# From the cross attention on: scheduler's order of the compute engines replaced by program order, with one list of weight splits

## The chip, the core and the metric

The kernel runs on one core of a Trainium2 chip. TensorE (PE) does the matmuls, VectorE (DVE), ScalarE (ACT) and GpSimd (POOL) the rest, and SyncE (SP) issues the loads. The metric is the device time of one execution in microseconds; the kernel before takes 1673.18 us (median of three runs, 1670.4 to 1673.23).

## What is computed

One layer of a first model and two layers of a second, on 256 tokens of width 1024, all in float32:

```python
# first block
y = concat(conformer_conv(p), rwkv7_mix(p)) @ w_out;          x = x + rms_norm(y, g1)
y = memory_cross_attention(rms_norm(x, g2), mem_n, wq, wkv, wo);  x = x + rms_norm(y, g3)
y = swiglu(rms_norm(x, g4), w_gu, w_down);                    x = x + rms_norm(y, g5)
# second block, layer 0 (mixer: moba attention) and layer 1 (mixer: mamba2)
x = x + 0.5 * swiglu(rms_norm(x, f1), gate, up, down)
x = x + mixer(rms_norm(x, mx))
x = x + 0.5 * swiglu(rms_norm(x, f2), gate, up, down)
```

So behind the first mixing come, in this order: cross attention, FFN (2816 wide), FFN, moba attention, FFN, FFN, mamba2, FFN. The mamba2 mixer projects to z and x (2048 each), B and C (1024 each) and 32 steps, runs a causal convolution of four taps and silu over x, B and C, a chunked scan of 32 heads in 8 groups, gates with silu(z), norms each group, and projects back.

## The kernel before, in words

**Matmuls and splits.** Each float32 product is made of three fp32r matmuls: high part by high part, high by low, low by high. So every weight unit (128x2048 float32, 1 MB) is loaded by SP into one of three raw buffers (pools `praw` and `pr8`) and split in two halves of 1024 columns: a cast on ACT into `wh` (L205, or L198 for units made `ahead`) and a subtraction on DVE into `wl` (L207, L199); some units of the mamba2 part subtract on POOL. The pool `pw` holds four halves; an `ahead` unit goes into two buffers of the pool of seven big tiles instead. Activations are split in the same way (`split`, L314 and L316).

**Order.** From the first weave on, PE's instructions are in program order (`manual_schedule` with PE alone). ACT, DVE, POOL and SP are ordered by the compiler's scheduler, which may put a later instruction first; `high_priority` marks those that it is to prefer.

**FFN.** `ffn` runs eleven chunks of 256 columns: eight steps of gate and up (`wide_step`, six 512-column matmuls, three for each half of the tokens), silu and product (`evict`, L1104 and L1105), four PE transposes of the chunk before (`turned`), and the down projection of the chunk before (`down_steps`). In chunks 0 and 10 the two halves of the tokens come one after the other.

**The boundary between two parts.** `down_two` does the last two down units, first for token half 0, then for half 1. `Fin.done(th, o)` adds the result to x: one DVE addition (L432) where there is no gain (`post` is None), or squares on ACT, a root on POOL and two products and two additions on DVE (L439 to L450) where there is one. `PreT.turn(th, q)` makes the next part's input: four PE transposes into one PSUM bank (L391), then for each of the four blocks a product on ACT (`xh`, L397) and a subtraction on DVE (`xl`, L398), then a square on ACT (L383). Half 0 is turned inside `down_two`; the two turns of half 1 (`late`) come in the next part, after its steps 1 and 3 (no gain) or 5 and 7 (gain), and at the very start of the mamba2 part.

**Weave.** `weave(fill, chains)` lays out attention and mixer: each step takes the next piece of the projections (`fill`), then one step of every chain that is due; a chain's `yield n` says after how many steps it goes on. In the mamba2 part a step of fill is twelve matmuls of 256 columns, and a group g starts eight steps after the group before it.

**A mamba2 group** (`group`): `conv_unit` (a product L1429 on DVE, two ACT products L1432, six DVE taps, L131), tanh (L1453) and a product (L1454), eight ACT relus and two exps (L1467, L1468) from PE's broadcasts, the masked B-C product (L1475 to L1479), the gate (L1484, L1485), PE transposes of x and the scaled copies (L1496 to L1499), PE's products with the masks (`by`) and the carried state (`bo`), sums (L1517 to L1520), squares (L1523), a root on POOL (L1524 to L1527), the norm on ACT (L1529), PE transposes of y (L1534), and the split of the result (L1540, L1541).

Of the kernel before, what the change touches and what calls it, by code (L numbers as in the profile page):

```python
# [97 lines left out]
def _build(ctx, nc, tc, a):  # L98
# [112 lines left out]

    def lin_step(bk, u, xh, xl, k, m, last=7):
        h, l = u
# [6 lines left out]
    def lin_pair(bks, us, xh, xl, k, last=7):  # L220

        for lo_ in (False, True):
# [17 lines left out]
    def linT_step(bk, u, xh, xl, k):  # L240
        h, l = u[0][k // 4], u[1][k // 4]
# [13 lines left out]
    def wide_step(bks, us, xh, xl, k, halves=(0, 1)):  # L255

        h, l = us[k // 4]
# [9 lines left out]
    def down_part(acc, u, hh, hl, th, o, k, first, last):  # L267
        t, c = slice(th * 128, th * 128 + 128), slice(o * 512, o * 512 + 512)
        h, l = u[0][k][:, c], u[1][k][:, c]
# [5 lines left out]
    def down_two(acc, u, yu, v, yv, fin):  # L275


        for th in range(2):
            hh, hl = yu(th)
            for o in range(2):  # L280
                for k in range(2):
                    down_part(acc, u, hh, hl, th, o, k, False, False)
            yield
            if th and fin.post is None:
                fin.turn(0, 0)
                fin.turn(0, 1)
            hh, hl = yv(th)
            for o in range(2):
# [3 lines left out]
                if th and fin.post is not None:  # L292
                    fin.turn(0, o)
                yield
# [179 lines left out]
    def weave(fill, chains):  # L474
# [4 lines left out]
        while due or fill:  # L479
            if fill and next(fill[0], "end") == "end":  # L480
                fill.pop(0)
                if fill:
                    continue
            left = []
# [8 lines left out]
            n += 1  # L493

# [453 lines left out]
    order.__enter__()  # L948
    yc = split(y_c[1])
# [3 lines left out]
    uq = unit(a["wq"][0]), unit(a["wq"][1])  # L953
# [5 lines left out]
    psa = mkpool("psa", 4, space=PSUM)  # L959

    def outs_of(n, l, get, nfs, nx, fins, nxt, post, acc):

        acc.extend(new_acc())
        for g in range(l - 2):
            yield from down_steps(acc, unit(a[n][g], True), lambda: get[g], g == 0)
        u, v = unit(a[n][l - 2], True), unit(a[n][l - 1], True)
        nfs.extend(two(*nx)())
        fins.append(Fin(xt, acc, nxt, post))
        yield from down_two(acc, u, lambda th: get[l - 2], v, lambda th: get[l - 1], fins[0])

    def two(n, l):
        return lambda: (unit(a[n][l * 22], True, ahead=True), unit(a[n][l * 22 + 1]))


    def softmax_T(bk, scale_ap):
# [18 lines left out]
    def first_heads():  # L994
        qb[0].append(bank())
        qb[1].append(bank())
        for k in range(8):
            lin_pair((qb[0][0], qb[1][0]), uq, xh, xl, k)
# [4 lines left out]
    def mem_head(h):  # L1003
# [7 lines left out]
        Pn = softmax_T(bk, r16)  # L1011
        yield 2
# [14 lines left out]
    acc, nf = [], []  # L1027
# [5 lines left out]
    def rope_tables():  # L1033
# [27 lines left out]

        ang = reduce_angle(ang, 2 * math.pi * 4096.0)
        ang = reduce_angle(ang, 2 * math.pi)
        rr = s1()[:, 0:128]
# [7 lines left out]
        S.activation(sn[:, 128:256], ab2, AF.Sin)  # L1072
        for n in ("qn", "kn"):
            cg = s1("v").rearrange("p (h t) -> p h t", h=2)
# [9 lines left out]
    for h in (2, 3):  # L1084
        fill.append(pieces(lambda h=h: unit(a["wq"][h], True), qb[h]))
    fill.append(outs_of("wo", 4, oh, nf, ("wgu", 0), fins, nxt2, "g3r", acc))
# [3 lines left out]
    def ffn(wgu, wd, l, pre, nf, before, nxt, post=None, ahead=None):  # L1090

# [6 lines left out]
        pend = None  # L1098
# [15 lines left out]
        last = []  # L1114

        def turned_last(th):
# [5 lines left out]
            with tc.high_priority():  # L1122
                split(bk[:, :, 0:128], "f", last[0][:, :, t], last[1][:, :, t])

        def gate_up(c):
            return unit(a[wgu][l * 22 + 2 * c], True, ahead=True), unit(a[wgu][l * 22 + 2 * c + 1], True)

        us10 = None
        for c in range(11):
            us = nf if c == 0 else us10 or gate_up(c)  # L1130
            b = bank(), bank()
            if c in (0, 10):
                for th in range(2):
                    for k in range(8):
                        wide_step(b, us, xh, xl, k, (th,))
# [6 lines left out]
                    if c == 0 and th == 0:  # L1142
                        r = pre.r()
                        ru = r
                        if post is None:
                            ru = small(2)
                            V.tensor_scalar(ru, r, 0.5, None, MUL)
                    evict(c, b[th], th)
            else:
                for k in range(8):  # L1150
                    wide_step(b, us, xh, xl, k)
# [4 lines left out]
            if c == 9:  # L1156
                us10 = gate_up(10)
            d = unit(a[wd][l * 11 + c], True)
            if 0 < c < 10:
                run(down_steps(acc, pend, lambda: hl, c == 1))  # L1160
            if c < 10:
                pend = d
        nf = ahead() if ahead else None
        fin = Fin(xt, acc, nxt, post)

        def last_but_one(th):
            if th:
# [3 lines left out]
        run(down_two(acc, pend, last_but_one, d, lambda th: last, fin))  # L1171
        return nf, fin
# [3 lines left out]
    nf, fin = ffn("wgu", "wdn", 0, pre, nf, fin, nx, "g5r", two("f1gu", 0))  # L1176
    pre, nx = nx, PreT("mx", 0)
    nf, fin = ffn("f1gu", "f1d", 0, pre, nf, fin, nx, None,
                   lambda: (unit(a["wqk"][0], True, ahead=True), unit(a["wqk"][1])))
# [64 lines left out]
    def pair(j):  # L1244
# [11 lines left out]
        for e in range(2):  # L1256
# [11 lines left out]
            S.activation(sm[:, 128:384], sm[:, 128:384], AF.Exp, bias=mx[:, 1:2], scale=SC, accum_out=su[:, 1:2])  # L1268
            V.reciprocal(su, su)
# [3 lines left out]
            yield E2 if e else 1  # L1273
# [25 lines left out]
    nf2, acc, fins = [], [], []  # L1299
    nx2 = PreT("f2", 0)  # L1300

    fill = [wide(lambda: nf, qk[0], late_, True)]
# [349 lines left out]
```

## Time and profile before

| | |
|---|---|
| median of three runs | 1673.18 us (1670.4 to 1673.23) |
| the profiled execution's own time | 1672.08 us |
| its span, first to last instruction | 1670.2 us |
| PE busy | 1605.0 us (96%) |
| DVE busy | 1062.8 us (64%) |
| ACT busy | 864.9 us (52%) |
| POOL busy | 148.5 us (9%) |
| mean granted PE clock | 0.988 |

Busy time is the union of an engine's instructions. A PE that is busy can run at the full clock of 2.4 GHz (1.00) or at half of it (0.50); the stretches at half clock are in the column PEclk of the windows. Parts, by the loads and lines of the trace: cross attention about 268 to 332 us, FFN to 527, FFN to 721, moba to 837, FFN to 1027, FFN to 1219, mamba2 to 1477, FFN to the end.

### The profile page before, as it was taken

To read this page: it belongs to the slowest core of one execution; us is meant where nothing else is said; L and a number is where in the kernel's file an instruction comes from. 1 tells how busy PE (TensorE), PEld (TensorE's weight loads), DVE (VectorE), ACT (ScalarE), POOL (GpSimd) and SP (SyncE) were. 2 spreads that over 40 slices of the span, in tenths; PEclk is the share of its full clock that TensorE was granted. 3 is DMA by queue.
4 is the path that set the end of the run, shared out by engine and by line. 5 is a ranking of instruction groups with operands and counts; after the bars stand their busy time and mean duration, and the time that the engine had idled before them with its cause. 6 is when DMAs were issued, how large, how long until landed. Compare 5 with 4: busy or idle time off the path is not lost.

```text
span 1670.2 us, 21978 instructions
## 1 busy us (share of the span) xinstructions
PE 1605.0 (96%) x8702; PEld 1374.4 (82%) x8702; DVE 1062.8 (64%) x1649; ACT 864.9 (52%) x1437; POOL 148.5 (9%) x162
## 2 busy tenths in 40 slices
PE   7999999999999999999999999999999888999999
PEld 7898988878887888877878887888898887778887
DVE  7888856655456555477565555555569888765454
ACT  6734446654345444466654445444466665554442
POOL 2322200000000000001000000000022433000000
PEclk9999999999999999999999999999999999999999
DMA  8321234354544445442454544545434322455442
GB/s 284 127 77 51 102 119 170 132 211 153 222 154 177 182 171 204 174 167 99 163 181 174 201 175 177 182 173 203 174 104 165 136 101 102 151 202 193 185 177 76
DMA packets 39846, 265.98 MB, mean 159 GB/s; under 512 B 4672, under 2 KB 5440, under 8 KB 8384
## 3 DMA queue, kind: packets, MB, share of 16 engines
q1 hardware_dynamic: 39456, 263.41, 43.4%
q8 instruction: 68, 1.11, 0.3%
q10 hardware_dynamic: 288, 1.18, 0.2%
q14 instruction: 34, 0.28, 0.1%
HBM read 263.52 MB, written 1.05 MB: 158 GB/s over the span
## 4 chain that ended last, share of the span: by engine, by line
PE 74%; DVE 14%; ACT 6%; issue 3%; POOL 1%; DMA 0%; SPq 0%; POOLq 0%; DVEq 0%; ACTq 0%
PE bk L181 71%; DVE wl L207 3%; DVE s2w L131 2%; ACT wh L205 2%; PE bk L1111 1%; DVE cv L131 1%; ACT s2w L1467 1%; DVE s2f L1519 1%; DVE s2f L1520 1%; ACT s L397 1%; PE bk L751 1%; PE bk L391 1%; DVE s2n L1429 1%; ACT s2w L1432 0%; DVE s L398 0%
## 5 line engine op out<-in xcount | busy, mean ns | idle before, releaser
L181 PE MATMUL bk<-wh,s 128*128 128x512 f32 (+1 forms) x2400 | 745.0, 384 | 14.7 <-ACT s L397 6.1
L207 DVE TENSOR_TENSOR wl<-raw,wh 128x1024 fp32r<-128x1024 f32 x344 | 422.7, 1234 | 265.7 <-ACT wh L205 264.9
L181 PEld LDWEIGHTS bk<-wh,s 128*128 128x128 f32 x2400 | 443.6, 191 | 108.3 <-DVE s L398 16.0
L205 ACT CAST wh<-raw 128x1024 fp32r<-128x1024 f32 x366 | 381.8, 1051 | 286.9 <-PE bk L181 266.4
L181 PE MATMUL bk<-wl,s 128*128 128x512 f32 (+1 forms) x1200 | 450.9, 376 | 1.3 <-POOL wl L207 1.3
L181 PE MATMUL bk<-wh,s2f 128*128 128x512 f32 x1072 | 345.6, 392 | 0.0
L181 PEld LDWEIGHTS bk<-wl,s 128*128 128x128 f32 x1200 | 229.2, 191 | 38.6 <-POOL wl L207 1.5
L181 PEld LDWEIGHTS bk<-wh,s2f 128*128 128x128 f32 x1072 | 201.2, 188 | 41.7 <-DVE s2f L316 0.2
L181 PE MATMUL bk<-s,wh 128*128 128x256 f32 x1120 | 217.6, 294 | 9.4 <-ACT wh L539 6.3
L181 PE MATMUL bk<-wl,s2f 128*128 128x512 f32 x536 | 208.7, 389 | 0.0
L181 PEld LDWEIGHTS bk<-s,wh 128*128 128x128 f32 x1120 | 178.0, 194 | 13.0 <-ACT wh L539 6.3
L199 DVE TENSOR_TENSOR wl<-raw,wh 128x1024 fp32r<-128x1024 f32 x120 | 144.2, 1220 | 51.3 <-ACT wh L198 50.7
L181 PE MATMUL bk<-s,wl 128*128 128x256 f32 x560 | 158.7, 287 | 4.2 <-DVE wl L207 3.9
L198 ACT CAST wh<-raw 128x1024 fp32r<-128x1024 f32 x120 | 123.5, 1052 | 46.7 <-DMA raw<-f1gu 19.8
L314 ACT CAST s2f<-bk 128x512 fp32r<-128x512 f32 (+1 forms) x64 | 35.3, 552 | 167.8 <-PE bk L1111 161.4
L316 DVE TENSOR_TENSOR s2f<-bk,s2f 128x512 fp32r<-128x512 f32 (+1 forms) x64 | 41.5, 649 | 126.2 <-ACT s2f L314 126.1
L181 PEld LDWEIGHTS bk<-wl,s2f 128*128 128x128 f32 x536 | 100.7, 188 | 20.3
L181 PEld LDWEIGHTS bk<-s,wl 128*128 128x128 f32 x560 | 108.5, 194 | 5.1 <-DVE wl L207 4.1
L331 POOL TENSOR_TENSOR sm<-sm,mh 128x2 f32<-128x2 f32 (+1 forms) x17 | 16.5, 971 | 786.7 <-DVE sm L330 786.7
L1104 ACT ACTIVATE s2w<-bk,sm 128x256 f32<-128x256 f32 x110 | 51.6, 474 | 41.0 <-PE bk L181 40.4
L1105 DVE SCALAR_TENSOR_TENSOR s2w<-bk,sm,s2w 128x256 f32<-128x256 f32 x110 | 52.6, 482 | 27.5 <-ACT s2w L1104 27.3
L207 POOL TENSOR_TENSOR wl<-raw,wh 128x1024 fp32r<-128x1024 f32 x22 | 56.9, 2602 | 83.1 <-ACT wh L205 71.6
(329 smaller groups left out, 1431.6 us busy)
## 6 DMA issues: line engine op xcount, KB each, us to landing
raw<-f1gu SPq DMA_DIRECT2D x44, 1024.0 KB, 4.8
raw<-f2gu SPq DMA_DIRECT2D x44, 1024.0 KB, 4.8
raw<-wgu SPq DMA_DIRECT2D x22, 1024.0 KB, 4.9
raw<-f1d SPq DMA_DIRECT2D x22, 1024.0 KB, 4.9
raw<-f2d SPq DMA_DIRECT2D x22, 1024.0 KB, 5.4
raw<-wxbc SPq DMA_DIRECT2D x16, 1024.0 KB, 4.8
raw<-wdn SPq DMA_DIRECT2D x11, 1024.0 KB, 6.2
raw<-win SPq DMA_DIRECT2D x10, 1024.0 KB, 4.9
```

Source lines behind the costliest of these rows:

```text
L131: V.scalar_tensor_tensor(o, src, w, o, MUL, ADD)
L181: PE.matmul(out, lhsT, rhs, start=start, stop=stop, skip_group_check=True)
L198: S.copy(h[:, c], r[:, c])
L199: V.tensor_tensor(l[:, c], r[:, c], f(h[:, c]), SUB)
L205: S.copy(h, r[:, c])
L207: (eng or V).tensor_tensor(l, r[:, c], f(h), SUB)
L314: S.copy(hh, src)
L316: V.tensor_tensor(hl, src, f(hh), SUB)
L391: PE.transpose(bk[:, i * 128:i * 128 + 128], xt[:, th, k * 128:k * 128 + 128], ident)
L397: S.mul(self.xh[:, k, t], b, pc(gname, gi + k))
L1104: S.activation(t, b[:, 0], AF.Silu, scale=r[:, th:th + 1])
L1105: V.scalar_tensor_tensor(t, b[:, 1], ru[:, th:th + 1], t, MUL, MUL)
```

## The change

From the end of the first mixing on, a second `manual_schedule` puts ACT, DVE and POOL in program order too; `high_priority` has no say there. SP stays with the scheduler. The weight units become objects in one list, in the order in which PE uses them. `feed()` emits the next half split of the list where it is called, unless four halves are alive (or an `ahead` unit is); `need()` forces splits that a matmul would otherwise lack, `done()` counts a half as dead at its last matmul. Calls of `feed` stand in the FFN's steps, in `down_two`, and after each step of `weave`. In `down_two` with a gain, both turns of half 0 now come after the first column half of token half 1.

In the mamba2 group the waits between steps change from 1, 1, 2, D0=2, D1=5, D2=11 (22 steps from its start to its end) to 1, 1, 1, 1, 1, 2, 1, 1, 2, 1 (12 steps); the convolution's taps come a step after its first products, the norm's root, product and transposes get steps of their own, and the product after tanh moves behind the first relus. `states` and the cross attention's softmax get one more step boundary, moba's waits E1 and E2 go from 3 and 6 to 2 and 4 with one boundary more, and the rope tables are cut into steps.

```diff
+    class Unit(list):
...
+        def cast(self):
...
+            S.copy(h, self.raw[:, c])
+            self.eng.tensor_tensor(l, self.raw[:, c], f(h), SUB)
...
+    def load_more():
+        while Plan.loaded < min(len(Plan.units), Plan.at + 3):
+            Plan.units[Plan.loaded].load()
+            Plan.loaded += 1
+
+    def feed():
+        if Plan.at == len(Plan.units):
+            return False
+        u = Plan.units[Plan.at]
+        if u.ahead and u.n == 0:
+            if Plan.ahead:
+                return False
+            Plan.ahead = 1
+        elif not u.ahead:
+            if Plan.live == 4:
+                return False
+            Plan.live += 1
+        load_more()
+        u.cast()
+        if u.n == 2:
+            Plan.at += 1
+            load_more()
+        return True
...
     def down_two(acc, u, yu, v, yv, fin):
         for th in range(2):
             hh, hl = yu(th)
+            if th:
+                feed()
             for o in range(2):
                 for k in range(2):
                     down_part(acc, u, hh, hl, th, o, k, False, False)
-            yield
+                if not th:
+                    feed()
+            yield False
             if th and fin.post is None:
                 fin.turn(0, 0)
                 fin.turn(0, 1)
+                feed()
             hh, hl = yv(th)
             for o in range(2):
                 for k in range(2):
                     down_part(acc, v, hh, hl, th, o, k, False, True)
                 fin.done(th, o)
-                if th and fin.post is not None:
-                    fin.turn(0, o)
-                yield
+                if th and o == 0 and fin.post is not None:
+                    fin.turn(0, 0)
+                    fin.turn(0, 1)
+                    feed()
+                yield False
+        feed()
...
     def weave(fill, chains):
...
+            if w is not False:
+                feed()
...
+    def plan_ffn(wgu, wd, l):
+        g = lambda c: (U(a[wgu][l * 22 + 2 * c], ahead=True), U(a[wgu][l * 22 + 2 * c + 1]))
+        d = lambda c: U(a[wd][l * 11 + c])
...
+    ubc = [U(a["wxbc"][8 + i], ahead=i == 0, eng=(V, G)[i > 1 and i % 2]) for i in range(8)]
+    uxz = [(U(a["wxbc"][g]), U(a["wz"][g], eng=G)) for g in range(8)]
...
+    rest = tc.manual_schedule(engines={mybir.EngineType.Activation, mybir.EngineType.DVE, mybir.EngineType.Pool})
+    rest.__enter__()
...
     def ffn(units, pre, before, nxt, post=None):
...
                     for k in range(8):
+                        feed()
                         wide_step(b, us, xh, xl, k, (th,))
...
+                    if c and th:
+                        feed()
+                        feed()
                     evict(c, b[th], th)
...
     def group(g):
-        xs = conv_unit(bx[g][0], 2 * g)
+        xs = yield from conv_unit(bx[g][0], 2 * g)
         th = s2("n")
         S.activation(th, xs, AF.Tanh, scale=0.5)
-        V.scalar_tensor_tensor(xs, th, 1.0, xs, ADD, MUL)
-        yield 1
...
-            yield 1 + pr
+            yield 1
+            if pr == 0:
+                V.scalar_tensor_tensor(xs, th, 1.0, xs, ADD, MUL)
...
-        for M in Ms:
-            V.tensor_tensor(M, M, bmid(CB[:, 0], 2), MUL)
-        yield D0
+        yield 1
...
-        yield D1
+        yield 2
...
+        yield 1
         for c in range(2):
             V.tensor_tensor(y4[:, c], by[c][:, :, 0:64], y4[:, c], ADD)
...
+        yield 1
         V.tensor_tensor(rs, rs, rq, MUL)
...
+        yield 2
         for c in range(2):
             S.mul(y[:, c], y[:, c], rs[:, c:c + 1])
-        yield D2
+        yield 1
```

## Rows read from the trace of the kernel before

**Rows 1.** Windows: stretch, its length, each engine's busy us, granted PE clock

```profile
400.00:500.00 100.00, 100.00 (x454) 82.73 (x453) 50.26 (x53) 43.51 (x52) 0.00 (x0) 1.00 0.51 189
332.00:347.00 15.00, 12.21 (x39) 7.70 (x37) 10.60 (x23) 9.61 (x23) 2.15 (x2) 0.77 0.68 245
1027.00:1037.00 10.00, 8.30 (x28) 5.20 (x27) 9.11 (x22) 8.38 (x20) 1.51 (x1) 0.83 0.58 211
1344.10:1363.90 19.80, 17.70 (x131) 17.26 (x131) 16.91 (x30) 12.10 (x29) 6.45 (x6) 0.91 0.30 107
1354.87:1356.30 1.43, 1.43 (x14) 1.43 (x13) 1.42 (x5) 0.24 (x2) 1.12 (x3) 1.00 1.01 430
1262.50:1269.20 6.70, 4.92 (x23) 4.92 (x24) 6.70 (x7) 2.94 (x5) 4.39 (x3) 0.50 0.00 0
```

**Rows 2.** Waits of PE: who for whom, us in total, times, longest

```profile
PE bk L181 <- DVE wl L207: 3.9, 1, 3.9
...
PE bk L1277 <- ACT s2f L1270: 2.0, 1, 2.0
```

**Rows 3.** The page's costliest groups: count, then busy and mean ns

```profile
L207 DVE TENSOR_TENSOR wl<-raw,wh 128x1024 fp32r<-128x1024 f32 x344 | 422.7, 1234 | 265.7 <-ACT wh L205 264.9
...
L205 ACT CAST wh<-raw 128x1024 fp32r<-128x1024 f32 x366 | 381.8, 1051 | 286.9 <-PE bk L181 266.4
```

**Rows 4.** Timeline of ACT, late turn at 539 us: start, length, idle before

```profile
538.93 0.37 ACT L397 ACTIVATE s<-bk,pk 128x128 fp32r<-128x128 f32 x1 [4.33 <-PE bk L391]
539.72 0.37 ACT L397 ACTIVATE s<-bk,pk 128x128 fp32r<-128x128 f32 x1 [0.42 <-DVE s L398]
```

**Rows 5.** Timeline of DVE, the same turn

```profile
539.33 0.35 DVE L398 SCALAR_TENSOR_TENSOR s<-bk,pk,s 128x128 fp32r<-128x128 f32 x1 [2.04 <-ACT s L397]
```

**Rows 6.** Timeline of PE at the boundary near 1027 us

```profile
1023.78 1.03 PE L391 MATMUL bk<-idt,s 128*128 128x128 f32 x8
...
1029.40 0.60 PE L391 MATMUL bk<-idt,s 128*128 128x128 f32 x4
```

**Rows 7.** Timeline of ACT at the same boundary

```profile
1027.91 0.61 ACT L397 ACTIVATE s<-bk,pk 128x128 fp32r<-128x128 f32 x2
1028.42 0.62 ACT L383 ACTIVATE s2n<-s 128x512 f32<-128x512 f32 x1
...
1029.03 0.36 ACT L397 ACTIVATE s<-bk,pk 128x128 fp32r<-128x128 f32 x1
```

**Rows 8.** Timeline of DVE at the same boundary

```profile
1026.70 0.68 DVE L432 TENSOR_TENSOR s<-s,bk 128x512 f32<-128x512 f32 x1
```

**Rows 9.** Timeline of ACT in one mamba2 group

```profile
1341.89 1.09 ACT L1432 ACTIVATE s2w<-s2n,pk 128x256 f32<-128x256 f32 x2 [1.38 <-DVE s2n L1429]
1342.89 1.37 ACT L1467 ACTIVATE s2w<-bk,acT 128x128 f32<-128x128 f32 x5
...
1345.41 0.66 ACT L1453 ACTIVATE s2n<-s2w 128x512 f32<-128x512 f32 x1
...
1353.11 0.42 ACT L1523 ACTIVATE s2c<-s2f 128x256 f32<-128x256 f32 x1 [4.57 <-DVE s2f L1520]
...
1356.10 0.91 ACT L1529 ACTIVATE s2f<-s2f,sm 128x256 f32<-128x256 f32 x2 [1.19 <-POOL sm L1527]
```

**Rows 10.** Timeline of DVE in the same group

```profile
1342.90 2.46 DVE L131 SCALAR_TENSOR_TENSOR s2w<-s2n,pk,s2w 128x256 f32<-128x256 f32 x6
...
1346.71 0.75 DVE L1517 TENSOR_TENSOR s2f<-bk,s2f 128x256 f32<-128x256 f32 x2
...
1347.83 2.46 DVE L1519 TENSOR_TENSOR s2f<-s2f,s1v 128x256 f32<-128x256 f32 x1
```

**Rows 11.** Timeline of POOL in the same group

```profile
1347.60 4.92 POOL L207 TENSOR_TENSOR wl<-raw,wh 128x1024 fp32r<-128x1024 f32 x2 [10.69 <-ACT wh L205]
```

**Rows 12.** Lines L1519 and L1520 over the whole span: ns min/median/max

```profile
L1519 DVE TENSOR_TENSOR s2f<-s2f,s1v x8: 419/2448/2467, 1312.0 to 1441.5; 128x256 f32<-128x256 f32 x8
...
L1520 DVE TENSOR_TENSOR s2f<-s2f,s2c x8: 691/1726/2767, 1314.5 to 1442.0; 128x512 f32<-128x512 f32 x8
```

More of the change, by code (lines that the diff above doesn't have):

```diff
@@ new lines, in _build, with U @@
+    class Plan:
+        units, at, loaded, live, ahead = [], 0, 0, 0, 0
+    def U(*args, **kw):
+        Plan.units.append(Unit(*args, **kw))
+        return Plan.units[-1]
+    def load_more():
[20 more added lines that the diff above has]
+        return True
@@ L212, in lin_step, with need, done @@
+    def need(u, i):
+        while isinstance(u, Unit) and u.n <= i:
+            assert feed()
+    def done(u, i):
+        if isinstance(u, Unit) and i not in u.dead:
+            u.dead.add(i)
+            if not u.ahead:
+                Plan.live -= 1
+            elif len(u.dead) == 2:
+                Plan.ahead = 0
     def lin_step(bk, u, xh, xl, k, m, last=7):
+        need(u, k // 4)
+        if m and k % 4 == 3:
+            done(u, k // 4)
         h, l = u
@@ L220, in lin_pair @@
     def lin_pair(bks, us, xh, xl, k, last=7):
+        for u in us:
+            need(u, k // 4)
+            if k % 4 == 3:
+                done(u, k // 4)
         for lo_ in (False, True):
@@ L240, in linT_step @@
     def linT_step(bk, u, xh, xl, k):
+        need(u, k // 4)
+        if k % 4 == 3:
+            done(u, k // 4)
         h, l = u[0][k // 4], u[1][k // 4]
@@ L255, in wide_step @@
     def wide_step(bks, us, xh, xl, k, halves=(0, 1)):
-        h, l = us[k // 4]
+        u, i = us[k // 4], k % 4 // 2
+        need(u, i)
+        if k % 2 and halves[-1]:
+            done(u, i)
+        h, l = u
         c = slice(k % 2 * 512, k % 2 * 512 + 512)
@@ L268, in down_part @@
         t, c = slice(th * 128, th * 128 + 128), slice(o * 512, o * 512 + 512)
+        need(u, k)
+        if th and o:
+            done(u, k)
         h, l = u[0][k][:, c], u[1][k][:, c]
@@ L479, in weave @@
         while due or fill:
-            if fill and next(fill[0], "end") == "end":
+            w = next(fill[0], "end") if fill else False
+            if w == "end":
                 fill.pop(0)
@@ L1097, in ffn @@
         ts = {}
-        pend = None
+        last = []
+        gu, dn = units
         def evict(c, b, th):
@@ L1121, in turned_last @@
                 PE.transpose(bk[:, i, 0:128], ts[10][:, th, i * 128:i * 128 + 128], ident)
[L1122 to L1128, printed above, removed]
+            split(bk[:, :, 0:128], "f", last[0][:, :, t], last[1][:, :, t])
+        hl = None
         for c in range(11):
-            us = nf if c == 0 else us10 or gate_up(c)
+            us = gu[c]
             b = bank(), bank()
@@ L1150, in ffn @@
                 for k in range(8):
+                    feed()
                     wide_step(b, us, xh, xl, k)
@@ L1155, in ffn @@
                     evict(c, b[th], th)
-            if c == 9:
-                us10 = gate_up(10)
-            d = unit(a[wd][l * 11 + c], True)
             if 0 < c < 10:
[L1160 to L1163, printed above, removed]
+                for _ in down_steps(acc, dn[c - 1], lambda: hl, c == 1):
+                    feed()
         fin = Fin(xt, acc, nxt, post)
@@ L1169, in last_but_one @@
             return hl
-        run(down_two(acc, pend, last_but_one, d, lambda th: last, fin))
-        return nf, fin
+        run(down_two(acc, dn[9], last_but_one, dn[10], lambda th: last, fin))
+        return fin
     pre, fin = nxt2, fins[0]
     nx = PreT("f1", 0)
-    nf, fin = ffn("wgu", "wdn", 0, pre, nf, fin, nx, "g5r", two("f1gu", 0))
+    fin = ffn(uf[0], pre, fin, nx, "g5r")
     pre, nx = nx, PreT("mx", 0)
-    nf, fin = ffn("f1gu", "f1d", 0, pre, nf, fin, nx, None,
-                   lambda: (unit(a["wqk"][0], True, ahead=True), unit(a["wqk"][1])))
+    fin = ffn(uf[1], pre, fin, nx)
     xh, xl = nx.xh, nx.xl
@@ L1432, in conv_unit @@
             S.activation(cur[:, m], pb[:, m, 0:256], AF.Identity, bias=pc("sb", t0 + m), scale=pc("sw", (t0 + m) * 4))
-            for j in range(1, 4):
+        yield 1
+        for j in range(1, 4):
+            for m in range(2):
                 tap(cur[:, m], pb[:, m, j:j + 256], pc("sw", (t0 + m) * 4 + j))
```

117 lines of the change are left out of this document (79 added, 38 removed).

## The prediction

> **What bounds the kernel now.** I read the page's busy times first, then the windows by stretch, then PE's waits, then the timelines of the stretches in which PE waits. PE is busy for 1605.0 of 1670.2 us, so at most 65 us of idle can be won, and what runs before the cross attention isn't touched. Inside an FFN there is nothing to win: PE is busy for 100.00 of 100 us at full clock, with DVE at 50.26 and ACT at 43.51 [rows 1]. PE waits at the boundaries, 2.79 us near 332 and 1.70 us near 1027 [rows 1]; in the mamba2 groups, 2.1 us of each 19.8 [rows 1]; and once each, 3.9 us for a split at 1260 and 2.0 us in moba [rows 2]. After such waits the granted clock falls to 0.50 for a while, the lower of its two levels, as in the last of [rows 1]: there PE works, at half pace.
>
> So the kernel is bound by PE, and the change moves only what PE waits for. The question is whether engines that run strictly in program order deliver in time what a free order delivered.
>
> **FFN bodies: 0.** The list holds per chunk six halves, 6 x 1.05 us on ACT and 6 x 1.23 us on DVE [rows 3], in the 17 us or so that PE needs for a chunk (an FFN of eleven lasts some 190). Walking through `feed`: the two `ahead` halves are emitted at steps 4 and 5 of a chunk, the next at step 6, the others in the down projection, each just behind the matmuls that free its buffer, and all of them most of a chunk before their use. That chunk of PE work hides them; without it each late half would cost some 2.3 us. The loads stay on SP, which isn't ordered, three units ahead for three buffers as now.
>
> **Boundaries without a gain: four times +3.3.** Emitted order at the end of `down_two`: turns (0,0) and (0,1), then `feed` (the next part's third half), then the matmuls whose sums `done` adds on DVE. So DVE has in its queue eight `xl`, the subtraction of that half, and only then the addition to x that the late turn waits for. Count from the start of the transposes. ACT and DVE take turns on one bank: ACT's next product waits for DVE, 0.79 us from one to the next [rows 4, 5]. First product at 0.63, fourth at 3.0; the square holds ACT, 0.86 from the last product to what follows (0.25 and 0.61 [rows 7]), so the second turn begins at 3.85 and the cast of the half at 7.1; the cast takes 1.05, the subtraction about 1.2 [rows 3], the addition 0.68 [rows 8]: 10.0 us. PE comes to the late turn at 5.62 in this trace, with 0.6 of that waiting [rows 6], so at 5.0. It waits 5.0 us where all waits here are 1.70 [rows 1], as they are at 721, 836 and 1477: 4 x 3.3 = 13. Bounds: if ACT and DVE overlapped fully in the turns, the wait would be 2.5 us (+0.8 each); behind a slower cast +5 each. I take +3.3, since rows 4 and 5 show the alternation.
>
> **Into the mamba2 part: +4.6.** There the late turns are PE's first work, 1.37 us earlier (two steps of three 512-column matmuls): a wait of 6.3 against 1.7.
>
> **Boundaries with a gain (332 and 527): twice +4.6.** The same queue, with ACT's square of the sum ahead of the turns. From the end of the first column half: products from 0.7, the cast at 7.2 to 8.2, its subtraction to 9.5. PE needs the half at 4.9 and its low part one matmul later: 3.3 and 1.0 us of waiting. Behind it on DVE stand the root and the products of token half 1; the late turn waits another 1.3, and the next half, behind those, 1.7. Together 7.3 against 2.79 [rows 1]: +9 for both. Bounds 0 to +7 each.
>
> **Into the cross attention: +1.** The first three casts of wq now follow in ACT's order what was there; if none can start early that is 3 x 1.05, if the scheduler lets them, nothing.
>
> **Cross attention heads and moba: 0.** Moba's 2.0 us wait [rows 2] may go with the shorter waits E1 and E2, and a softmax split in steps blocks less; against it DVE's rope products (some 5 us in a row) now stand in front of splits. From -4 to +8; I take the middle of the small effects, none.
>
> **Start of mamba2: +3.** The split that PE waited 3.9 us for [rows 2] stands in the list behind the taps of four B and C units (4 x 2.46 [rows 10]), the run of small steps for the decay, and two products: about 7 us late. From -3.9 (the wait goes) to +6.
>
> **The groups: 8 x +2.6.** This decides. A group now passes from its products `by` to its PE transposes of y in five steps instead of eleven. PE's own work in between is five steps of 1.43 [rows 1] and about 1.4 of small products: 8.6 us. The path, in the emitted order: four sums and products on DVE, 0.75 for two [rows 10], 0.4, and the shortest of L1519 and L1520, 0.42 and 0.69 [rows 12]: 2.3; two squares on ACT 0.8; then, because they stand ahead in the queues, the next group's first products on ACT 1.0 from 1341.89 to 1342.89 [rows 9], a cast 1.05, which DVE awaits for its subtraction 1.2, then the six taps 2.5 [rows 10], for which ACT's tanh 0.66 waits, eight relus and two exps 3.2 (2.52 to 1345.41, and the second exp) [rows 9], a cast for POOL 1.05, and at last the norm 0.9 [rows 9]. Sum 14.7, with hand-overs of some 0.03 [rows 4, 5] 15.0 us. PE waits 6.4 us. Its work per group is 17.70 us, 1.8 of them due to the clock at 0.91 over 19.8 [rows 1]: 15.9. So a group takes 22.4 us where it took 19.8: +21 us. Bounds: at PE's own pace -3.8 each; if the long sums stay long (2.46 and 2.76), +6.7 each.
>
> **Clock: +4.** Mean clock 0.988 is a loss of 20 us. Longer waits at the same places bring about as many half-speed stretches, some longer; from -8 to +25.
>
> Sum: 13 + 4.6 + 9 + 1 + 0 + 3 + 21 + 4 = 56 on the profiled execution's 1672.08, so 1728; the median of the runs lies 1.1 above it: 1729 us.
>
> **Rivals.** *The groups run at PE's pace (faster).* Place: DVE in the group. In this trace the sums L1519 and L1520 take 2.46 and 2.76 us while POOL's two z splits run, 4.92 us [rows 10 to 12], and 0.42 and 0.69 at best. The new list puts z splits after the group's third and fifth step, away from these sums: 4.1 us of DVE time back per group. If that, and not the queue order, is what set the 19.8 us, groups fall to 15.9: 8 x -3.9 = -31, the wait at 1260 and the half clocks of the part go too, -9, and with the boundaries' +27 the time is 1659; 1632 if the boundaries keep their present waits. Decision point: the path of 15.0 us must come under 8.6. For it: the blocked sums are the largest removable item in DVE's 16.91 us. Against it: 15.0 is counted with these sums already short. Chance 0.22.
>
> The Trainium skill (SBUF — State Buffer, section "Who interferes with whom") states that a VectorE operation with two SBUF inputs and a GpSimd operation that reads SBUF exclude each other for the whole instruction. This trace agrees: 2.46 us beside POOL, 0.42 without. By that rule alone the change gains, and 1642 would be the time; by the queues it loses.
>
> *Balance.* The groups gain a little or nothing and the boundaries lose by their lower bounds: 1669 to 1700. Chance 0.10, of which 0.04 within 0.2%.
>
> *The clock decides.* Every wait of 5 us or more starts a half-speed stretch as at 1262 [rows 1], 6.7 us long and 3.4 us dear: sixteen of them, half hidden in the waits, make +27 instead of +4: 1752. Rows against it: after the 2.1 us waits of the groups it came in some groups only. Chance 0.20.
>
> **How the numbers follow.** The forecast (1700 to 1745) has 0.48. What can be told from no change is 0.2%. Faster 0.22, same 0.04, slower 0.74. The range leaves out the two ends, the groups and the boundaries both at their best (under 1645) and the clock at its worst (over 1765), some 0.1 each; the forecast's own range is 1700 to 1745.
>
> **What would show it.** Right: in a window of 10 us at each boundary one wait of PE of about 5 us for the addition L432, behind a subtraction; in the groups PE waiting some 6 us at the transposes of y for ACT's norm; ACT idle before tanh for DVE's taps; L1519 near 0.42. The FFN windows stay at 100. Wrong: groups of 16 to 19 us, or boundary waits under 2 us; then the queues keep up, because a split stands elsewhere than I count it or the engines overlap more than rows 4 and 5 show.

## The result and the profile after

The changed kernel takes 1792.99 us (median of four runs, 1791.95 to 1793.7) against 1672.84 us for the kernel before in the same comparison: a ratio of 1.0721, 95% interval 1.0702 to 1.0740. The forecast was 1729 us (1700 to 1745; with the rivals the range ended at 1765). The direction was right, and the waits named at the boundaries and in the groups came; the size was half of what came: +120 us were measured, +56 forecast.

Both kernels issue the same 8702 PE instructions in nearly the same order, so the two profiled executions can be laid side by side from one PE instruction to the same one. The spans are 1670.2 and 1791.9 us. PE's idle time grew from 65.2 to 152.0 us; the time at half clock within the span grew from 39 to 143 us, and half of the part of it in which PE worked (what that work would save at full clock) from 17.2 to 57.1 us. By stage, in us:

| stretch between the same PE instructions | before | after | more | predicted |
|---|---|---|---|---|
| cross attention | 92.9 | 98.3 | +5.4 | +1 |
| two boundaries with a gain, with their FFNs | 388.0 | 397.0 | +9.0 | +9 |
| four boundaries without a gain (first 9 to 19 us) | 47.4 | 61.3 | +13.9 | +13 |
| into the mamba2 part | 8.6 | 15.6 | +7.0 | +4.6 |
| moba behind its late turn | 104.8 | 126.8 | +22.0 | 0 |
| mamba2 to the first group's transposes of x | 70.1 | 100.4 | +30.3 | +3 |
| groups, from there to the last transposes of y | 145.9 | 180.5 | +34.6 | +21 |
| clock, counted by itself in the prediction | | | in the rows above | +4 |

The page of the changed kernel, for [rows 3], has the same cost of one split (the counts differ because these lines now make all splits):

```profile
L233 DVE TENSOR_TENSOR wl<-raw,wh 128x1024 fp32r<-128x1024 f32 x420 | 506.0, 1230 | 256.7 <-ACT wh L232 256.5
L232 ACT CAST wh<-raw 128x1024 fp32r<-128x1024 f32 x442 | 454.3, 1049 | 189.1 <-PE bk L181 187.7
```

Its windows, for [rows 1] (stretch, length, busy us of PE, PEld, DVE, ACT, POOL, granted PE clock, DMA share, GB/s): the middle of an FFN, a boundary without a gain, the half-speed stretch behind the next such boundary, one settled mamba2 group, moba, and the first steps of mamba2.

```profile
600.00:700.00 100.00, 100.00 (x452) 82.70 (x451) 53.11 (x54) 44.92 (x54) 0.00 (x0) 1.00 0.52 185
876.90:890.20 13.30, 8.42 (x29) 6.66 (x28) 7.45 (x16) 7.59 (x19) 0.00 (x0) 0.74 0.22 79
1075.90:1082.70 6.80, 5.91 (x18) 4.94 (x19) 4.39 (x10) 2.81 (x8) 0.00 (x0) 0.50 0.44 154
1417.50:1441.30 23.80, 18.05 (x130) 17.53 (x130) 13.35 (x28) 12.43 (x29) 6.38 (x6) 0.86 0.27 92
752.00:876.90 124.90, 107.96 (x478) 86.14 (x476) 76.08 (x151) 68.25 (x148) 8.91 (x5) 0.93 0.34 127
1280.10:1380.50 100.40, 75.56 (x524) 71.80 (x522) 62.06 (x116) 44.81 (x73) 22.67 (x19) 0.86 0.27 96
```

The FFN is as full as before. In the last three no engine is full: PE waits while DVE and ACT are busy for 45 to 62% of the time. PE's waits, for [rows 2] (who for whom: us in total, times, longest):

```profile
PE bk L1662 <- ACT s2f L1657: 40.5, 8, 5.6
PE bk L487 <- DVE s L528: 25.8, 5, 6.3
PE bk L181 <- ACT wh L232: 17.0, 8, 5.6
PE bk L181 <- POOL s2n L1548: 9.6, 6, 2.2
PE bk L181 <- DVE wl L233: 9.4, 13, 1.3
PE bk L181 <- ACT s2c L1358: 7.2, 3, 3.1
```

The first line is the groups' transposes of y behind the norm (seven times 5.64 us, once 1.05), the second the late turns behind the addition to x. Where the second comes from is seen near 877 us on DVE (compare [rows 5, 8]) and ACT (compare [rows 4, 7]) (start, length, instruction, idle time before it):

```profile
876.36 0.35 DVE L494 SCALAR_TENSOR_TENSOR s<-bk,pk,s 128x128 fp32r<-128x128 f32 x1 [0.52 <-ACT s L493]
...
878.72 0.35 DVE L494 SCALAR_TENSOR_TENSOR s<-bk,pk,s 128x128 fp32r<-128x128 f32 x1 [0.43 <-ACT s L493]
880.26 1.22 DVE L233 TENSOR_TENSOR wl<-raw,wh 128x1024 fp32r<-128x1024 f32 x1 [1.19 <-ACT wh L232]
881.40 1.27 DVE L528 TENSOR_TENSOR s<-s,bk 128x512 f32<-128x512 f32 x2
```

```profile
878.32 0.37 ACT L493 ACTIVATE s<-bk,pk 128x128 fp32r<-128x128 f32 x1 [0.42 <-DVE s L494]
...
879.19 1.98 ACT L232 CAST wh<-raw 128x1024 fp32r<-128x1024 f32 x2
```

The products of the turn alternate at 0.79 us, then come the cast, the subtraction, and only then the two additions; PE, free at 877.26, goes on at 882.1.

In a settled group the chain of work between two transposes of y closes on itself, 23.7 us once round (start, length, engine and line; compare [rows 9, 10]):

```profile
1422.92 1.30 PE bk L1662 x4
...
1427.60 4.45 PE bk L181 x38
...
1433.65 0.70 DVE s2f L1646
...
1434.43 0.91 ACT s2c L1649 x4
1435.35 0.98 ACT s2w L1552 x2
1436.33 0.95 ACT wh L232
1437.28 0.02 issue
1437.31 1.23 DVE wl L233
...
1438.81 2.38 DVE s2w L131 x6
1441.18 0.02 issue
1441.20 0.63 ACT s2n L1576
...
1445.12 1.03 ACT wh L232
1446.15 0.42 ACT s2f L1657
```

From the end of PE's products (1432.04) it runs over sums, squares, the next group's products, a cast, its subtraction, the taps, tanh, relus, a cast and the norm to 1446.61: 14.6 us. The sums are short in all eight groups, as [rows 12] were only at best (ns min/median/max):

```profile
L1645 DVE TENSOR_TENSOR s2f<-s2f,s1v x8: 424/426/427, 1386.0 to 1553.6; 128x256 f32<-128x256 f32 x8
...
L1646 DVE TENSOR_TENSOR s2f<-s2f,s2c x8: 691/692/693, 1386.4 to 1554.0; 128x512 f32<-128x512 f32 x8
```

### The profile page after: what moved, and what is told of

It reads as the page before. It is cut to its first block, busy times and chain, and to the rows that moved or that the text cites. A ratio compares the mean times of both kernels' runs of the same rounds, so it can differ in the third digit from the quotient of the medians.

```text
span 1791.9 us, 22067 instructions
## 1 busy us (share of the span) xinstructions
PE 1639.9 (92%) x8702; PEld 1406.6 (78%) x8702; DVE 1059.1 (59%) x1649; ACT 867.7 (48%) x1435; POOL 141.5 (8%) x162
## 3 DMA queue, kind: packets, MB, share of 16 engines
HBM read 263.52 MB, written 1.05 MB: 148 GB/s over the span
## 5 line engine op out<-in xcount | busy, mean ns | idle before, releaser
L233 DVE TENSOR_TENSOR wl<-raw,wh 128x1024 fp32r<-128x1024 f32 x420 | 506.0, 1230 | 256.7 <-ACT wh L232 256.5
L232 ACT CAST wh<-raw 128x1024 fp32r<-128x1024 f32 x442 | 454.3, 1049 | 189.1 <-PE bk L181 187.7
L181 PEld LDWEIGHTS bk<-wh,s 128*128 128x128 f32 x2400 | 448.6, 193 | 92.2 <-ACT wh L232 11.5
L181 PE MATMUL bk<-wl,s 128*128 128x512 f32 (+1 forms) x1200 | 456.5, 380 | 9.1 <-DVE wl L233 7.1
L181 PE MATMUL bk<-s,wh 128*128 128x256 f32 x1120 | 232.0, 307 | 16.4 <-ACT wh L232 7.4
L181 PEld LDWEIGHTS bk<-s,wh 128*128 128x128 f32 x1120 | 189.8, 207 | 20.4 <-ACT wh L232 8.1
L181 PE MATMUL bk<-s,wl 128*128 128x256 f32 x560 | 165.7, 299 | 8.0 <-POOL s2n L1548 5.4
L181 PEld LDWEIGHTS bk<-s,wl 128*128 128x128 f32 x560 | 115.0, 205 | 10.6 <-POOL s2n L1548 6.4
L493 ACT ACTIVATE s<-bk,pk 128x128 fp32r<-128x128 f32 x128 | 46.2, 366 | 73.8 <-DVE s L494 37.2
L494 DVE SCALAR_TENSOR_TENSOR s<-bk,pk,s 128x128 fp32r<-128x128 f32 x128 | 44.2, 350 | 62.6 <-ACT s L493 62.5
L1231 ACT ACTIVATE s2w<-bk,sm 128x256 f32<-128x256 f32 x110 | 52.2, 474 | 59.8 <-PE bk L181 57.1
```

What stands on the lines that cost most here:

```text
L181: PE.matmul(out, lhsT, rhs, start=start, stop=stop, skip_group_check=True)
L232: S.copy(h, self.raw[:, c])
L233: self.eng.tensor_tensor(l, self.raw[:, c], f(h), SUB)
L493: S.mul(self.xh[:, k, t], b, pc(gname, gi + k))
L494: V.scalar_tensor_tensor(self.xl[:, k, t], b, pc(gname, gi + k), f(self.xh[:, k, t]), MUL, SUB)
L1231: S.activation(t, b[:, 0], AF.Silu, scale=r[:, th:th + 1])
```

## Which part of the change costs

Ratios are to the kernel before, timed on the same chip in the same comparison; the changed kernel stands at 1.0721. "Group" is the settled distance from one group's tanh to the next (before: 15.8, 17.0, 18.8, then 19.76 us, 18.66 on average; after: 23.85 us settled, 23.49 on average).

| kernel | us | ratio | 95% interval | group |
|---|---|---|---|---|
| order of ACT, DVE, POOL free | 1666.99 | 0.9962 | 0.9948 to 0.9976 | 17.1 |
| only POOL in order | 1663.19 | 0.9937 | 0.9917 to 0.9957 | 17.1 |
| free, and the mixers' old steps | 1677.01 | 1.0028 | 1.0013 to 1.0043 | 19.75 |
| only ACT in order | 1741.20 | 1.0412 | 1.0393 to 1.0431 | 22.2 |
| only DVE in order | 1722.19 | 1.0299 | 1.0279 to 1.0319 | 19.0 |

**Order free.** Edit:

```diff
-    rest = tc.manual_schedule(engines={Activation, DVE, Pool})
-    rest.__enter__()
...
-    rest.__exit__(None, None, None)
```

> The changed kernel with the order of ACT, DVE and POOL left free again; the list of splits and the short steps of the mixers stay. Theory: the strict order of the queues makes the waits, and each wait brings a half-speed stretch, so without it the boundary waits of 4.9 us fall to about 2 us, the waits of 5.6 us at the transposes of y and those in the first steps of mamba2 go, and the time is 1670 to 1720 us. Rival: the short steps and the places of the splits on the list make the loss by themselves (a split that stands late on the list is late in any order): 1760 us or more.

It came to 1666.99 us: the list and the short steps don't lose, the strict order does, 126 us of it. One window of a settled group in this kernel:

```profile
1336.20:1353.30 17.10, 16.11 (x130) 15.61 (x130) 15.35 (x29) 11.93 (x29) 6.72 (x7) 1.00 0.36 125
```

PE is busy for 16.1 of 17.1 us at full clock, and DVE for 15.4.

**One engine in order.** Edits: the same line with one engine in the set.

> The changed kernel with ACT alone (and PE, as ever) in program order; DVE and POOL free. Theory: the long waits end at ACT (casts that stand behind an exponential or a relu that waits, the norm of y behind the next group's products, relus and cast), so ACT's order alone costs most of the 126 us between the free order and the strict one: 1730 to 1780 us. Rival: each queue waits for the other, and the loss needs both: under 1700 us.

> The changed kernel with DVE alone (and PE) in program order; ACT and POOL free. Theory: at the boundaries the addition to x still stands behind the subtraction of a split, so the waits there keep 2.5 to 5 us, while in the groups ACT can take the norm first: 1685 to 1720 us. Rival: DVE's order is the whole loss (six taps in front of what ACT waits for): 1750 us or more.

> The changed kernel with POOL alone (and PE) in program order; ACT and DVE free. Theory: POOL has some 4 instructions per group and little to be late with: 1665 to 1675 us. Rival: the memset of each convolution behind POOL's split of 2.4 us (waits of 1.7 to 2.0 us of PE in the first steps of mamba2, some 10 us in all) remains: 1677 to 1690 us.

ACT alone costs 74 us over the free order, DVE alone 55, POOL nothing (its 4 us less than the free order lie within the two intervals). 74 and 55 make 129, nearly the 126 of all three; for DVE the theory expected a little less. But the sums agree by luck: stage by stage they don't. Between the same PE instructions, the strict order loses against the free one 18.9 us in moba, 26.4 in the first steps of mamba2, 7.3 on the way into mamba2 and 51.6 in the groups. ACT's order alone loses 8.4, 6.3, 7.1 and 38.3 there, DVE's alone 1.3, 9.4, 6.6 and 15.7. In the groups the two nearly add up, into mamba2 either alone does the harm, and in moba and the first steps of mamba2 the two together lose far more than their sum. With ACT in order a group waits for the norm (six waits of up to 4.2 us), with DVE in order it hardly does (0.9 at most; second window: 16.56 of 19.00 us busy, clock 1.00):

```profile
1377.27:1399.82 22.55, 18.36 (x139) 17.71 (x138) 14.59 (x31) 13.13 (x31) 7.32 (x6) 0.92 0.30 101
```

```profile
1373.83:1392.83 19.00, 16.56 (x134) 15.77 (x132) 14.45 (x28) 11.80 (x30) 6.45 (x6) 1.00 0.31 112
```

The first steps of mamba2 take 70.1 us before, 74.0 in the free order, 80.3 with ACT and 83.4 with DVE in order, 100.4 after. About 4 us of the difference to before (70.1 to 74.0) are not a matter of the order: PE waits for the product after the first group's tanh, 0.8 us before, 5.9 in the changed kernel and nearly as long in the free order with the same steps (first line: changed, second: free).

```profile
PE bk L1612 <- DVE s2w L1593: 5.9, 1, 5.9
```

```profile
PE bk L1610 <- DVE s2w L1591: 5.3, 1, 5.3
```

**List alone.** The old functions of the mixers and D0 to D2, E1, E2 as before, in the free order.

> The kernel with the order of ACT, DVE and POOL free, with the list of splits at fixed places, but with the mixers' steps as they were before (long steps, D0 to D2 = 2, 5, 11 and E1, E2 = 3, 6). It tells which part of the change gives the 7 us that the free order with list and short steps is faster than before. Theory: the short steps (sums away from POOL's splits, groups of 17.1 us instead of 19.8) give them, so this kernel takes 1672 to 1682 us. Rival: the list gives them: 1660 to 1668 us.

The list alone doesn't make the kernel faster (+0.3%); the short steps bring 10 us in the free order. In the traces the groups are 19.5 us shorter with them (128.9 for 148.4), and other stages, moba above all (107.9 for 103.5), give a part back. The gain stands where the rival on the groups expected it: with the old steps the sum takes 2.33 us in the median beside POOL's splits, with the new ones 0.43.

```profile
L1630 DVE TENSOR_TENSOR s2f<-s2f,s1v x8: 424/2330/2472, 1308.7 to 1443.0; 128x256 f32<-128x256 f32 x8
```

The Trainium skill (SBUF — State Buffer, section "Who interferes with whom") says that a VectorE operation with two SBUF inputs and a GpSimd operation that reads SBUF exclude each other; the trace agrees, with 2.33 us for 0.43. A settled group is 2.7 us shorter with the new steps. How much of that is due to these sums is not shown, since the short steps change the rest of the group too; in the strict order the queues take more than that back.

## Can a wait be repaired in the strict order?

Six edits of the changed kernel, all queues in order, each at the place where PE waits longest.

| edit | us | ratio | 95% interval |
|---|---|---|---|
| transposes of y four steps later | 1803.58 | 1.0780 | 1.0764 to 1.0796 |
| split behind the additions | 1794.06 | 1.0716 | 1.0697 to 1.0736 |
| E0, E1, E2 = 9, 3, 6 | 1792.79 | 1.0713 | 1.0695 to 1.0731 |
| memset on DVE | 1790.83 | 1.0702 | 1.0686 to 1.0718 |
| convolutions behind the decay | 1794.39 | 1.0725 | 1.0709 to 1.0741 |
| norm of y written earlier | 1802.68 | 1.0784 | 1.0763 to 1.0805 |

**A longer tail.** In `group`, behind the norm:

```diff
             S.mul(y[:, c], y[:, c], rs[:, c:c + 1])
-        yield 1
+        yield 5
```

> The changed kernel with one number changed: the transposes of y come 5 steps behind the norm instead of 1 (4 steps of 1.43 us of PE work more in front of them). Theory: the seven waits of 5.64 us are a matter of too few steps; with them their half-speed stretches of 6.8 us go (2 us of loss each): between 35 and 54 us less, 1739 to 1758 us, and a group takes 16 to 18 us instead of 23.85. Rival: ACT's and DVE's queues are full in a group, and the wait only moves to another place (products CB or by): less than 10 us gained, 1783 us or more.

A miss: the seven waits for the norm went, and a group took 25.3 us instead of 23.85. The wait stands in two new places, the transposes of x and the products with the scaled x:

```profile
PE bk L1612 <- DVE s2w L1593: 25.3, 7, 6.0
...
PE bk L181 <- DVE s2w L1620: 10.4, 7, 2.9
```

**Split behind the additions.** In `down_two`, the `feed()` behind the two early turns moves to the end:

```diff
                 fin.turn(0, 1)
-                feed()
...
+        feed()
         feed()
```

> The changed kernel with the split between the early turns and the additions moved behind the additions, at every boundary between parts. Theory: the cast and the subtraction (2.3 us together) are what the addition waits for beyond the turns, so the five waits of 4.9 to 6.3 us fall by 2.0 to 2.3 us each, and the two boundaries with a gain by about as much; with what the half-speed stretches give back, 1774 to 1782 us. Rival: the split is only late at another place, since PE needs its half some steps later: 1790 to 1796 us.

The price of the step is as predicted, and about half of it is given back at other places. The late turn now waits 2.5 us instead of 4.9:

```profile
886.87 0.65 PE L486 MATMUL bk<-idt,s 128*128 128x128 f32 x4 [2.50 <-DVE s L527]
```

Counted until PE's instructions keep a constant distance again, the four boundaries without a gain are 2.4, 2.7, 2.8 and 1.4 us shorter, and the way into mamba2 1.0. But the split is late for what follows: the two boundaries with a gain are 3.3 and 1.7 us longer, moba 1.1. From the end of the cross attention on the trace is 4.7 us shorter; ahead of the changed stages, where the edit does nothing, it is some 3 us longer, and the median of four runs shows no gain.

**Moba's waits.** `E0, E1, E2 = 7, 2, 4` becomes `9, 3, 6`.

> The changed kernel (all queues in order) with longer waits in moba: E0, E1, E2 = 9, 3, 6 in place of 7, 2, 4. Theory: the short waits are what PE waits for there (7.2 us for the copies after the transposes of q and k, 2.9 us for the softmax): without them and the half-speed stretches that follow 12 to 18 us less, 1774 to 1781 us. Rival: ACT's and DVE's queues are late as a whole in this part (rope products in front of splits), and the waits move: 1787 us or more.

Three waits of 7.2 us for the copies became two of 13.1; moba gained 2.5 of the 22 us it lost:

```profile
PE bk L181 <- ACT s2c L1358: 13.1, 2, 9.7
```

**Memset.** `G.memset` in `conv_unit` becomes `V.memset`.

> The changed kernel with the memset of each convolution on DVE instead of POOL. Theory: on POOL it stands behind a split of 2.4 us, and the product, the two products of ACT and the next cast wait for it; the waits at the next halves go from 1.7 to 2.0 us to under 1 in the first steps of mamba2, and a group loses a wait too: 5 to 12 us less, 1781 to 1788 us. Rival: PE waits there for POOL's split itself, whatever stands behind it: 1791 us or more.

The rival was right about the cause (its time, 1791 us or more, was met within the spread of the runs). The profile names the releaser whose semaphore came last, here the memset behind POOL's split; without it the wait is that for the split, as long as before (7.6 us for 7.4 in the same stretch):

```profile
PE bk L181 <- POOL wl L233: 7.6, 4, 2.1
```

**Convolutions behind the decay.** In the list of chains:

```diff
-(11, states(0)), (11, states(1))] + [(3 + 4 * i, states(i)) for i in range(2, 8)]
+(14, states(0)), (15, states(1)), (16, states(2))] + [(3 + 4 * i, states(i)) for i in range(3, 8)]
```

> The changed kernel with the first three convolution units of mamba2 started at steps 14, 15 and 16 instead of three at once at step 11: their 18 taps in a row (7.21 us on DVE) no longer stand ahead of the decay's exponential, for which ACT's next cast waits. Theory: PE's wait of 5.59 us at 1307 us goes, with the 10.2 us at half speed behind it: 8 to 11 us less, 1782 to 1785 us. Rival: the taps are only late at another place: 1790 us or more.

In the changed kernel ACT's queue is held for 9.0 us by the decay's exponential, behind DVE's 18 taps:

```profile
1308.68 0.26 ACT L1491 ACTIVATE sm<-sm 128x64 f32<-128x64 f32 x1 [9.00 <-DVE sm L1489]
```

```profile
1300.86 7.21 DVE L131 SCALAR_TENSOR_TENSOR s2w<-s2n,pk,s2w 128x256 f32<-128x256 f32 x18
```

With the edit the taps come later, and PE waits before them for the product of the convolution, which now stands behind the decay's small steps on DVE. One stretch is 10.0 us shorter, the one before it 8.1 us longer:

```profile
PE bk L181 <- DVE s2n L1549: 6.2, 1, 6.2
```

**Norm of y written earlier.** The scale follows the squares at once, the norm's products one step later, ahead of the next group's taps and relus; PE's order stays.

```diff
             S.activation(zs[:, c], y[:, c], AF.Square, accum_out=rs[:, c:c + 1])
-        yield 1
...
         G.tensor_tensor(rs, rs, rh, MUL)
-        yield 2
+        yield 1
         for c in range(2):
             S.mul(y[:, c], y[:, c], rs[:, c:c + 1])
-        yield 1
+        yield 3
```

> The changed kernel (all queues in order) with the norm of y written earlier: its scale right behind the squares, its two products on ACT one step later, ahead of the next group's taps, tanh, relus and cast; the transposes of y stay at the same step of PE. Theory (the loss in the groups is the place in the queue, not the strict order as such): the path from the products by to the norm falls from 14.5 us to about 6, under PE's 9.2 us, the seven waits of 5.64 us go, a group takes 18 to 20 us instead of 23.7: 1755 to 1775 us. Rival (ACT and DVE go round taking turns, whichever instruction stands first): the waits move to the products of the next group, as they did with the longer tail, and the time stays at 1785 us or more.

A miss again, in favour of the rival: the waits at the transposes of y are gone, and PE waits for the scaled x and at the transposes of x instead; a group takes 24.6 us. The edit isn't a clean test, though: the next group's product on DVE, which in the changed kernel ran as the sums ended, now stands behind the scale's steps and POOL's memset and starts 2.6 us after the sums (at 1439.02 for 1436.43). Without these 2.6 us a group would take 22.0 us (an estimate), still more than the 18 to 20 expected.

```profile
PE bk L181 <- DVE s2w L1620: 22.5, 7, 4.4
PE bk L1612 <- ACT s2w L1588: 12.9, 7, 2.2
```

```profile
1435.74 0.69 DVE L1646 TENSOR_TENSOR s2f<-s2f,s2c 128x512 f32<-128x512 f32 x1
...
1439.02 0.69 DVE L1549 TENSOR_TENSOR s2n<-bk,s1k 128x512 f32<-128x512 f32 x1 [1.19 <-POOL s2n L1548]
```

None of the six moved the time by more than 0.2% to the good. As the chains read, what sets the pace in the mixers is not a single wait but the round: in the strict order ACT's cast stands behind an activation that waits for DVE, DVE's subtraction stands behind that cast, and both stand ahead of what PE needs next. No run took the casts and subtractions out of the round while the queues stayed in order, so this is read from the traces and not shown by a run.

## What the half clock costs

**PE kept at work in its waits.** Two kernels put work without use in front of the transposes; first only in the groups (all eight), then in seven groups and at the five boundaries without a gain.

```diff
         bk = bank()
+        for _ in range(46):
+            mm(bk[:, 0], ahl[:, 0:128], ahl, True, True)
         for i in range(2):
             for c in range(2):
                 PE.transpose(bk[:, i, c * 128:c * 128 + 128], ...)
```

> The changed kernel with 46 matmuls of 256 columns (about 5.5 us of PE work at full clock) put in front of each group's transposes of y; their result is overwritten by the transposes and not used. They fill the wait of 5.64 us. Theory: the half-speed stretch comes from the wait, so with PE at work there it does not come: some 2 us less per group, 1776 to 1784 us, and a granted clock of 1.00 behind the transposes. Rival: the stretches have nothing to do with the wait, or come with the amount of work: 1793 us or more, clock at 0.50 as now.

> The changed kernel with PE work that fills its waits and has no other use: 46 matmuls of 256 columns in front of the transposes of y in the first seven groups, and 23 transposes of the identity in front of the late turn at the five boundaries without a gain. Theory: the half-speed stretches behind those waits are a cost of their own: 1.6 to 3.0 us at each of the five boundaries and some 0.8 us in each group, so 1776 to 1781 us. Rival: they cost nothing, because what PE does at half speed is waited for by nobody: 1791 us or more.

The first took 1796.37 us (1.0732, 1.0716 to 1.0748), the second 1787.69 us (1.0689, 1.0671 to 1.0706), 0.3% under the changed kernel with intervals that overlap a little. The 9 to 17 us expected of the first and the 12 to 17 of the second did not come. In the traces the clock does what was expected: in the groups no stretch at half clock is left, and a group takes 22.85 us instead of 23.85 with 46 matmuls more:

```profile
1418.97:1441.82 22.85, 21.89 (x179) 21.21 (x178) 13.40 (x28) 12.34 (x29) 7.38 (x6) 1.00 0.27 93
```

The first kernel gives the 5.4 us that its groups gained in the trace back, mostly because in the eighth, where PE had waited only 1.0 us, the filling costs 4.3 us more than the wait did; besides, 2.1 us lie ahead of the changed stages. So of the 2.06 us that half speed costs PE in a group, 1.0 costs time. The rest passed in a wait: at full clock PE comes to the product with the carried state sooner and waits there for 0.75 us, which it did not at half clock, because POOL's scaling of x for that product stands behind a split (chain of the first kernel):

```profile
1428.61 2.39 POOL wl L233
1431.00 1.55 POOL s1v L1624
...
1432.61 0.71 PE bk L181 x2
```

In the second kernel the boundaries near 877, 1071 and 1265 us became 1.6, 1.2 and 0.8 us shorter and the other two did not; 23 transposes filled only 2.5 of the 4.9 us. Its seven groups gained 5.5 us, of which 1.7 were lost again in the eighth.

**The best of both.** The free order with POOL in order, E1, E2 = 3, 6, groups two steps later, transposes of y one step later:

> The version with ACT and DVE free and POOL in order, and three numbers more: E1, E2 = 3, 6 as before the change, the transposes of y one step later, the groups two steps later (37 + 8g). Theory: the waits that are left in the free order with short steps are a matter of single steps: moba gets back 2.5 us, the transposes of y 0.9 us in each of seven groups, the first group some 3 of its 5.3 us: 1650 to 1657 us. Rival: in a group DVE with 15.4 us of 17.1 is nearly as full as PE, so the waits move: 1660 to 1664 us.

1670.13 us (0.9989, 0.9974 to 1.0005): a miss, for the rival's range too. Of the waits that were left, the first group's fell from 5.3 to 3.5 us, but the settled groups went from 17.1 to 18.0 us, with DVE nearly as full as PE. The fastest version is the one with the list, the short steps, and only POOL (and PE) in order: 1663.19 us; the free order, 1666.99, can't be told from it.

## Why the prediction was wrong in size

- *FFN bodies: 0.* Right: 100.00 of 100 us.
- *Boundaries without a gain, +3.3 each.* Right in queue and size: waits of 4.88 to 4.91 us where 5.0 was predicted, +3.5 on average with the clock. *Into mamba2*: wait 6.26 for 6.3, but +7.0 for +4.6, since 2.9 us of half speed came with it.
- *Boundaries with a gain, +4.6 each.* Right in sum, +9.0, and partly by luck: PE idled 5.1 and 5.6 us where 7.3 was predicted, and half speed for 10.2 us at each, where it had been 6.8, made up some of the rest.
- *Cross attention, +1 and 0.* Small miss: +5.4; a wait of 2.6 us for a copy on ACT (L1127) and 3.4 us at half clock behind it were not in the sum.
- *Moba: 0 (from -4 to +8).* This step failed: +22. It priced the single wait of 2.0 us of [rows 2] and one series of rope products, and took "the middle of the small effects, none". The rows of before were those of a free order, in which DVE and ACT do what is ready. In the strict order DVE and ACT took turns waiting: 76 and 68 us busy in 125, PE idle for 17. The free order with the same steps loses only 3.1 of the 22 us; 18.9 are the order's, and they need both queues (8.4 with ACT's alone, 1.3 with DVE's).
- *Start of mamba2: +3 (from -3.9 to +6).* This failed most: +30.3. The mechanism was named (the split behind the taps and the decay's steps, wait 5.59 us), but counted once; the round of cast, POOL's split, product, taps and silu went on for six more units, with waits of 0.7 to 2.0 us, and what half speed costs there grew by 8 us (10.5 for 2.5). Not in the sum at all was the first group's wait after tanh, 5.9 us for 0.8, which comes with the short steps.
- *Groups: 8 x +2.6.* The wait was right (5.64 us, forecast 6.4), and so was the path (14.6 for 15.0), though with the norm taken out of that path a group took no less (24.6 us), so other chains are nearly as long. The term was 14 us too small: the base of 19.8 us was one settled group, where the mean was 18.66; PE's 7.3 us (15.9 less 8.6) between the transposes of y and the end of the products took 9.1, at half clock up to 1427; with the filling, at full clock, PE came to the product behind them after 8.2 us, 0.75 of them a wait, instead of 9.2.
- *Clock: +4.* Mis-sized. Behind the waits of 4.9 to 6.3 us came 3.4 to 6.8 us at half clock, behind that of 5.59 us 10.2, as *the clock decides* had it. Its price by the filling is 1.0 us per group and 0 to 1.6 us per boundary, near that rival's +27 in place and below it in size; most of the missing 64 us are moba (22), the start of mamba2 (27) and the groups (14).
- *The groups run at PE's pace* did not happen, but its mechanism exists: in the free order the short sums give groups of 17.1 us.

Open: whether another program order could be as good as the free one. Writing the free order out by hand was not tried; six local repairs say only that these single moves don't find it. In what part moba and the first steps pay for the clock was not measured either.

## What to carry to other kernels

A trace of a free order shows which waits are left, not which the scheduler has hidden: before the order is fixed by hand, walk each queue through a whole round of a stage, and ask whether the round ACT, DVE, ACT is longer than PE's work; by the chains that is what set the pace here (23.7 us for a group with 16.1 us of PE work). Count a change of order by rounds times repetitions, not by the one wait that the old trace shows. And change the work (short steps, sums away from POOL's splits) apart from the order: here the one gained 10 us and the other lost 126. Count what one queue's order costs stage by stage as well: two queues can lose together what neither loses alone.

## What was not expected of the hardware

Work without use made a stage faster: 46 matmuls more per group, 1.0 us less (granted clock 1.00 instead of 0.86). And POOL's split holds up a small DVE operation with one tensor input as well, not only sums of two tensors: this step of 64 elements, 0.19 us elsewhere, lasted until the split beside it ended. The section of the Trainium skill named above counts `tensor_scalar` among the operations that can contend with GpSimd when their operands meet certain conditions; the trace agrees, with 2.26 us.

```profile
1313.23 2.26 DVE L1506 TENSOR_SCALAR sm<-sm 128x64 f32<-128x64 f32 x1
```

```profile
1312.98 2.42 POOL L233 TENSOR_TENSOR wl<-raw,wh 128x1024 fp32r<-128x1024 f32 x1 [22.61 <-ACT wh L232]
```
